# A decoder block on one core: twelve early chunks in the first FFN, activations made ahead of their step, low parts of weighted sums last, and two POOL products on VectorE

## The chip, the cores and the metric

One core of one Trainium2 chip. The metric is the device time of one launch in microseconds, given as the median of several runs. Smaller is better.

## The reference

One layer of a decoder block on 256 tokens of width 2048, in float32. Everything is computed from `x`, a condition `c` and weights:

```python
ada = silu(c) @ w_ada + b_ada          # nine rows of 2048: shift, scale and gate of three sub-layers
h = rms_norm(x) * g * (1 + sc1) + sh1
x = x + 0.5 * gt1 * ((silu(h @ w_gate) * (h @ w_up)) @ w_down)      # first FFN, inner width 5632
u = rms_norm(x) * g * (1 + sc2) + sh2
q, kv, gate_logits, q_r, k_r, v_r, g_r, ga, gb = split(u @ w_in)
merged = sigmoid(ga) * (nsa(q, kv, gate_logits) @ w_proj_nsa) \
       + sigmoid(gb) * (retention(q_r, k_r, v_r, g_r) @ w_proj_ret)
x = x + gt2 * (merged @ w_out)
# second FFN like the first, with sh3, sc3, gt3
```

`nsa` is attention of 16 heads in 4 groups with compressed, selected and window branches; `retention` has 8 heads with 128x256 states, a normalisation over each head's 256 values and a gate `silu(g_r)`.

## The kernel before

Products are made in two parts each: a float32 matrix is split into a high part (`whi`, `ahi`, rounded by ScalarE) and a low part (`wlo`, `alo`, the difference, made by VectorE), and three matmuls add high·high, high·low and low·high. Weights come as tiles of two blocks of 128 rows by 512 columns, 512 KB each. One such tile is a **unit**: `unit` (or the body of `early`) multiplies it with the two halves of the 256 tokens in 12 matmuls of 128x512 (lines 235 to 237, in the early steps 681 to 683).

All loads stand in one written-out list, the **stream**, of weight tiles ("w") and of tiles of `w_ada` ("a"). `run` walks the list. SP issues the loads in that order into six `raw` buffers; a buffer comes free when its tile is prepared. `prep` prepares a tile up to `AHEAD` = 4 stream items before its turn: for "w" ScalarE makes `whi` (line 136) and VectorE `wlo` (line 137), with four buffers of each; for "a" VectorE multiplies by a condition column and adds (line 368, 16 such tiles make the sums of one slice). An item "do" runs a function at its place; a "bar" holds preparation back until the walk has reached it. `push` and `soon` put small pieces into a queue of which one is run after each unit.

The scale and shift of the first FFN come from `w_ada`, so its activations are not known at the start. The kernel therefore goes through the inner dimension in four **steps** (`STEPS`) of four blocks of 128. Step i needs the scale and shift of its own four blocks only. In each step the first `EARLY` = 9 chunks (gate and up chunks in turn, 512 columns each, two units per chunk and step) are taken as far as the step goes; ScalarE takes their sums out of PSUM (line 694) and puts them back before the next step's part (`seed`, line 700). The sums of chunks 0 to 7 lie in buffers of activations, later ones in `t4` buffers, of which there are six. The 16 "a" tiles of the next step are interleaved with the units of this one, by `SPREAD` = 0.95 over the first 17 of 18 units. At the end of that list stand `turn` (transposes of the normalised `x`, line 777), the sums over partitions with a vector of ones (`done`, line 403), and `mk`, which makes the step's activations: two ScalarE activations per block (lines 796 and 797) and VectorE's low part (line 800).

Ahead of the first step, TensorE runs a few matmuls whose results are not used (`with_raw`, `warm`).

Chunks that are not early, and all later matrices, run through `chunk` over the whole inner dimension. In attention, `pv` multiplies the values with the turned weights; the weights' low parts come from `p_tr` (line 1132, VectorE). In retention, `y` normalises a head's output and multiplies it with the gate (line 1235, POOL); `y_tr` transposes it (line 1248). In the merge, `b_done` multiplies (line 1302, VectorE) and adds (line 1303, POOL); `merge` then transposes the sum (line 473, a helper).

Of the kernel before, what the change touches and what calls it, by code (L numbers as in the profile page):

```python
# [29 lines left out]
O_KV, O_GL = 2048, 5120  # L30
O_QR, O_KR, O_VR, O_GR, O_GA, O_GB = 5168, 6192, 7216, 9264, 11312, 13360

RAW, PREP, AHEAD, T4, T2, EARLY, SPREAD = (6, 4, 4, 6, 8, 9, 0.95)
SLOPES = [2.0 ** (-8.0 * (i + 1) / HEADS) for i in range(HEADS)]


LEAD = (0, 0)
BAR = 1
WARM = (10, 15, 4)
FILL = (4, 40, 320, 50, 60, 10)  # L40
SLOW = 6
HOLD = (2,2,1)
# [26 lines left out]
def block_kernel(ctx: ExitStack, tc: tile.TileContext, I, konst, decay, out):  # L69
# [10 lines left out]
    def act_hi(dt=F32R):  # L80
        return ap_.tile([P, 4, S], dt, tag="ahi", name="ahi")
# [57 lines left out]
    def run():  # L139
# [55 lines left out]
        for it in items:  # L195
            kind = it[0]
            if kind == "do":
                it[1]()
                continue
            if kind == "bar":  # L200
                bars.pop(0)
                few = SLOW if len(it) > 2 else 0
                continue
            done = 0
            while st["prep"] < len(stream) and st["prep"] <= at + AHEAD and (not bars or st["prep"] < bars[0]):
                nxt = st["prep"]
                if nxt not in raws or (stream[nxt][0] == "w" and st["w"] >= nw - len(held) + PREP):
                    break
                if few and done == 2:
                    break  # L210
                done += stream[nxt][0] == "w"
                prep()
            few = max(few - 1, 0)
            while late_lo and late_lo[0][0] <= at and kind == "w":
                next_lo()
            if kind == "w":
                it[4](*parts.pop(at))
                nw += 1
# [164 lines left out]
        nc.tensor.matmul(ps, ones_r, by_turns(lo[:, i]), start=False, stop=True)  # L383
        return halves(ps)

    def ada_cols(lay, k0, nk=4, first=False):

        ks = slice(k0, k0 + nk)

# [7 lines left out]
            nc.vector.scalar_tensor_tensor(o[:, 1], o[:, 1], 1.0, g_norm[:, lay, ks], op0=ALU.add, op1=ALU.mult)  # L397

        def done(acc):
            if first:  # L400
                ps = mx()
                for k in range(2 * nk):
                    nc.tensor.matmul(ps[:, k:k + 1], acc[:, k * P:(k + 1) * P], ones[:, 0:1], start=True, stop=True)
                finish(ps[:, 0:2 * nk].rearrange("p (i k) -> p i k", i=2))
                return
            hi, lo = in_parts(acc)

            def f():
# [219 lines left out]
    def ffn(l, his, los, last, first=None, head=None):  # L628
# [79 lines left out]
        if first:  # L708
            its += first(*STEPS[0])
            for i, (k0, nk) in enumerate(STEPS):  # L710
                nxt = [None if i == 0 else ci for ci in range(1, EARLY)] + [0 if i + 1 < len(STEPS) else None]
                w = [it for ci in range(EARLY) for it in early(ci, k0, nk, nxt[ci])]
                if i + 1 < len(STEPS):
                    w = interleave(w, first(*STEPS[i + 1]), int(len(w) * SPREAD), *LEAD)
                its += w
        def both(c):
            g = [] if first and 2 * c < EARLY else chunk(act, src(wg, c), KT, NCH, gate_done(c), head=None if c else head)
# [33 lines left out]
    h1, l1 = [], []  # L751

    def first(k0, nk):
        banks = []

        def scaled(ks):
            for t in range(2):
                nc.scalar.activation(xs[:, t, ks], x[:, t, ks], AF.Copy, scale=rx[:, t:t + 1])

        def warm():  # L760
            ps = mx()
# [3 lines left out]
        def with_raw(raw):  # L765
            nc.tensor.matmul(mx(), ones, raw[:, :NCH], start=True, stop=True)

        def turn():

            ks = slice(k0 * P, (k0 + nk) * P)  # L770
            if k0 == 0:
                scaled(ks)
            for k in range(nk):
                if k % 2 == 0:
                    banks.append(mx([P, 2, S]))
                for t in range(2):
                    nc.tensor.transpose(banks[-1][:, k % 2, t * P:(t + 1) * P],
                                        xs[:, t, (k0 + k) * P:(k0 + k + 1) * P], ident)
            if k0 == 0:
                for n in range(1, 4):  # L780
                    scaled(slice(n * NCH, (n + 1) * NCH))

        def mk():
            n = 1 if k0 == 0 else 2
            if k0 == 0:
                warm()
            for k in range(0, nk, n):
                h32 = t2([P, 2, S])
                for i in range(n):
                    kt = k0 + k + i  # L790
                    if kt % 4 == 0:
                        h1.append(act_hi())
                        l1.append(act_lo())
                    a, b = mod[:, 1, kt:kt + 1], mod[:, 0, kt:kt + 1]
                    xT = banks[(k + i) // 2][:, (k + i) % 2]
                    nc.scalar.activation(h1[-1][:, kt % 4], xT, AF.Identity, scale=a, bias=b)
                    nc.scalar.activation(h32[:, i], xT, AF.Identity, scale=a, bias=b)
                next_lo()
                ks = slice((k0 + k) % 4, (k0 + k) % 4 + n)
                nc.vector.tensor_tensor(l1[-1][:, ks], h32[:, :n], h1[-1][:, ks].bitcast(F32), op=ALU.subtract)  # L800
        o = ada_cols(0, k0, nk, True)
        if k0 == STEPS[1][0]:
            o.insert(5, ("do", load_more))
        if k0 == 0:
            then = {0: lambda raw: small_cols(), 2: lambda raw: rms_first(), 3: lambda raw: turn()}
            then.update({i: with_raw for i in range(*WARM[:2])})
            for i, f in then.items():
                o[i] = (*o[i][:4], lambda raw, f=f, g=o[i][4]: (g(raw), f(raw)))
            o = [("do", lambda: [square(t, n, xs[:, t, n * NCH:(n + 1) * NCH]) for t in range(2) for n in range(4)])] + o
            return o + [("do", mk), ("bar", BAR)]  # L810
        o.insert(len(o) - 1, ("do", turn))
        return o + [("do", mk)]

    def squared(xa, rs):
        def f(t, n):
# [166 lines left out]
    def attention(g):  # L982
# [153 lines left out]
        def pv(t, brs, cmp_):  # L1136
            def f():
# [1 line left out]
                if start:  # L1139
                    box["o", t] = mx()  # L1140
                ps = box["o", t]
                for br in brs:
                    for j in range(t + 1):
                        ph, pl = box["pT", br, t, j]
                        vh, vl = box["v"][:, 0, j, br], box["v"][:, 1, j, br]
                        nc.tensor.matmul(ps, vh, ph, start=start, stop=False)
                        nc.tensor.matmul(ps, vh, pl, start=False, stop=False)
                        nc.tensor.matmul(ps, vl, ph, start=False, stop=False)
                        start = False
                if cmp_:  # L1150
                    nc.tensor.matmul(ps, vc[0:CMP, g, :], by_turns(box["pcT"][0:CMP, t]), start=False, stop=True)
# [27 lines left out]
    def retention(qd):  # L1179
# [35 lines left out]
        def y(h):  # L1215
            def f():
# [15 lines left out]
                for t in range(2):  # L1232
                    nc.vector.tensor_scalar(yn[:, t], ps[:, t], mv[:, t, 0:1], rs[:, t:t + 1],
                                            op0=ALU.subtract, op1=ALU.mult)
                nc.gpsimd.tensor_tensor(yn, yn, G[:, :, vh], op=ALU.mult)
                box["y", h] = yn
            return f

# [58 lines left out]
    def b_done(n):  # L1297
        def f(ps):
            g = sgb.pop(n)
            a = A[0][:, :, n * NCH:(n + 1) * NCH]  # L1300
            for t in range(2):
                nc.vector.tensor_tensor(in_two(g[:, t]), halves(ps[t]), in_two(g[:, t]), op=ALU.mult)
            nc.gpsimd.tensor_tensor(a, a, g, op=ALU.add)  # L1303
        return f

    for n in range(4):
# [58 lines left out]
```

## Time and profile before

| | us |
|---|---|
| median of 3 runs | 2477.15 (2477.02 to 2477.69) |
| the profiled execution, its own time | 2472.4 |
| its span, first to last instruction | 2470.6 |
| PE busy | 2428.3 |
| PE's weight loads busy | 2113.0 |
| DVE (VectorE) busy | 1742.2 |
| ACT (ScalarE) busy | 1202.1 |
| POOL (GpSimd) busy | 169.9 |

All rows and times inside the kernel are of the one profiled execution and count from its span's start. Matmuls are pipelined: a row's duration overlaps the next, so the spacing of starts tells the pace. "Idle before" is the time in which an engine did nothing before an instruction, with what ended it.

### The profile page before, as it was taken

The numbers are of one execution on the slowest core, as the hardware profiler recorded it, in microseconds if no ns is written. First come the engines' busy times: TensorE is split into PE (matmuls) and PEld (weight loads), VectorE is DVE, ScalarE is ACT, GpSimd is POOL, SyncE is SP. The second block draws the span as 40 slices with busy tenths as digits, with TensorE's granted clock in tenths as the row PEclk, the third lists the DMA queues.
The fourth block names the chain that finished last, engine by engine and source line by source line (L and its number), as shares of the span: only waits on it lengthen the run. The fifth ranks groups of instructions, "written<-read, shape, count | busy, mean of one in ns | idle before, by whom it ended". The sixth has DMA issues, their size and how long they took to land. (4 is left out here: it accounts for less than half of the span.)

```text
span 2470.6 us, 31644 instructions
## 1 busy us (share of the span) xinstructions
PE 2428.3 (98%) x11614; PEld 2113.0 (86%) x11614; DVE 1742.2 (71%) x2032; ACT 1202.1 (49%) x1548; POOL 169.9 (7%) x146
## 2 busy tenths in 40 slices
PE   6999999999999999999999999999999999999999
PEld 4888888888888888888888888888888888888887
DVE  7887768998756478886667777777788555555555
ACT  4677444434445455564444444445644444444443
POOL 1000000110000111100000101001000010001001
PEclk9999999999999999999999999999999999999999
DMA  9998888899876455668888787886599666666664
GB/s 352 353 355 293 279 296 296 310 318 343 273 229 203 140 155 160 204 203 272 281 267 256 253 254 254 274 271 232 176 348 325 200 203 203 196 200 202 202 199 152
DMA packets 348264, 616.65 MB, mean 250 GB/s; under 512 B 22096, under 2 KB 79926, under 8 KB 347852
## 3 DMA queue, kind: packets, MB, share of 16 engines
q1 hardware_dynamic: 347852, 614.51, 75.6%
q8 instruction: 91, 1.49, 0.2%
q14 instruction: 65, 0.53, 0.1%
q0 software_dynamic: 256, 0.12, 0.0%
HBM read 612.45 MB, written 2.10 MB: 249 GB/s over the span
## 5 line engine op out<-in xcount | busy, mean ns | idle before, releaser
L137 DVE TENSOR_TENSOR wlo<-raw,whi 128x1024 fp32r<-128x1024 f32 x852 | 1059.2, 1251 | 575.5 <-ACT whi L136 570.7
L136 ACT ACTIVATE whi<-raw 128x1024 fp32r<-128x1024 f32 x852 | 894.7, 1056 | 946.1 <-PE accb L237 717.3
L235 PE MATMUL accb<-whi,ahi 128*128 128x512 f32 x3168 | 1211.8, 383 | 1.3 <-ACT ahi L530 0.9
L236 PE MATMUL accb<-wlo,ahi 128*128 128x512 f32 x3168 | 1201.9, 379 | 1.5 <-DVE wlo L179 0.9
L237 PE MATMUL accb<-whi,alo 128*128 128x512 f32 x3168 | 1201.6, 379 | 0.0
L236 PEld LDWEIGHTS accb<-wlo,ahi 128*128 128x128 f32 x3168 | 599.0, 189 | 87.8 <-DVE wlo L179 3.8
L237 PEld LDWEIGHTS accb<-whi,alo 128*128 128x128 f32 x3168 | 598.7, 189 | 87.3 <-DVE alo L549 1.7
L235 PEld LDWEIGHTS accb<-whi,ahi 128*128 128x128 f32 x3168 | 598.9, 189 | 84.9 <-ACT ahi L530 2.0
L368 DVE SCALAR_TENSOR_TENSOR aacc<-raw,cond,aacc 128x1024 f32<-128x1024 f32 x270 | 353.9, 1311 | 1.4 <-DMA raw<-in_w_ada_dram 0.4
L619 POOL TENSOR_TENSOR x<-x,t 128x512 f32<-128x512 f32 x50 | 80.8, 1636 | 1396.6 <-DVE t L614 1001.0
L682 PE MATMUL accb<-wlo,ahi 128*128 128x512 f32 x288 | 112.4, 390 | 3.0 <-DVE wlo L137 3.0
L683 PE MATMUL accb<-whi,alo 128*128 128x512 f32 x288 | 109.7, 381 | 2.1 <-DVE alo L800 2.1
L681 PE MATMUL accb<-whi,ahi 128*128 128x512 f32 x288 | 110.3, 383 | 0.2
L682 PEld LDWEIGHTS accb<-wlo,ahi 128*128 128x128 f32 x288 | 54.6, 190 | 17.7 <-DVE wlo L137 10.9
L683 PEld LDWEIGHTS accb<-whi,alo 128*128 128x128 f32 x288 | 54.6, 189 | 10.3 <-DVE alo L800 3.3
L681 PEld LDWEIGHTS accb<-whi,ahi 128*128 128x128 f32 x288 | 54.7, 190 | 8.9 <-ACT whi L136 1.0
L598 DVE TENSOR_TENSOR alo<-mx,ahi 128x512 fp32r<-128x512 f32 x52 | 33.5, 686 | 29.3 <-ACT ahi L597 29.1
L597 ACT ACTIVATE ahi<-mx 128x512 fp32r<-128x512 f32 x52 | 28.2, 595 | 48.9 <-PE mx L473 48.9
L614 DVE TENSOR_TENSOR t<-accb,gt 128x512 f32<-128x512 f32 x56 | 36.5, 684 | 9.0 <-PE accb L237 9.0
L640 ACT ACTIVATE t<-accb 128x512 f32<-128x512 f32 x44 | 26.2, 600 | 27.2 <-PE accb L237 22.9
L868 ACT ACTIVATE t<-accb 128x512 f32<-128x512 f32 x44 | 25.9, 596 | 23.3 <-PE accb L237 23.3
L1108 ACT ACTIVATE t<-t,m 128x256 f32<-128x256 f32 (+1 forms) x64 | 28.2, 444 | 18.4 <-DVE m L1099 18.4
(200 smaller groups left out, 1052.9 us busy)
## 6 DMA issues: line engine op xcount, KB each, us to landing
raw<-in_w_ada_dram SPq DMA_DIRECT2D x288, 512.0 KB, 5.5
raw<-in_w_ffn_gate_dram SPq DMA_DIRECT2D x176, 512.0 KB, 5.0
raw<-in_w_ffn_up_dram SPq DMA_DIRECT2D x176, 512.0 KB, 4.7
raw<-in_w_ffn_down_dram SPq DMA_DIRECT2D x176, 512.0 KB, 4.4
raw<-in_w_in_dram SPq DMA_DIRECT2D x176, 512.0 KB, 4.5
raw<-in_w_in_dram SPq DMA_DIRECT2D x128, 256.0 KB, 3.9
raw<-in_w_proj_nsa_dram SPq DMA_DIRECT2D x32, 512.0 KB, 5.4
raw<-in_w_proj_ret_dram SPq DMA_DIRECT2D x32, 512.0 KB, 5.3
```

Source lines behind the costliest of these rows:

```text
L136: nc.scalar.activation(hi_ap, raw_ap, AF.Copy)
L137: nc.vector.tensor_tensor(lo_ap, raw_ap, hi_ap.bitcast(F32), op=ALU.subtract)
L235: nc.tensor.matmul(ps[t], xh, wh, start=kt == 0, stop=False)
L236: nc.tensor.matmul(ps[t], xh, wl, start=False, stop=False)
L237: nc.tensor.matmul(ps[t], xl, wh, start=False, stop=kt == K - 1)
L368: nc.vector.scalar_tensor_tensor(box[0], raw, k, box[0], op0=ALU.mult, op1=ALU.add)
L598: nc.vector.tensor_tensor(lo[:, 2 * b:2 * b + 2], ps, h.bitcast(F32), op=ALU.subtract)
L614: nc.vector.tensor_tensor(in_two(y), halves(ps[t]), in_two(gt[:, n * NCH:(n + 1) * NCH]), op=ALU.mult)
L619: engine.tensor_tensor(xs, xs, y, op=ALU.add)
L681: nc.tensor.matmul(ps[t], xh, wh, start=kt + a == 0, stop=False, **kw)
L682: nc.tensor.matmul(ps[t], xh, wl, start=False, stop=False, **kw)
L683: nc.tensor.matmul(ps[t], xl, wh, start=False, stop=kt + a == k0 + nk - 1, **kw)
```

## The change

Six edits. (1) `EARLY` goes from 9 to 12. (2) The "a" tiles of the next step are spread over all but the last `REST` = 4 units of a step. (3) `mk` is gone: in steps 1 to 3 the activations are made in pieces that `soon` runs after the following units, and the scaling of `x` and its transposes (`turn`) stand after the 8th and 12th "a" tile. (4) In the first step the activations are made block by block with one stream item prepared between two blocks (the new item "prep"). One more `with_raw` is issued. (5) `pv` takes high·high and low-value·high of all tiles first and the products with the weights' low parts last. (6) The product with the gate in `y` and the sum in `b_done` are issued to VectorE instead of POOL.

```diff
-RAW, PREP, AHEAD, T4, T2, EARLY, SPREAD = (6, 4, 4, 6, 8, 9, 0.95)
+RAW, PREP, AHEAD, T4, T2, EARLY, REST = (6, 4, 4, 6, 8, 12, 4)
-WARM = (10, 15, 4)
+WARM = (10, 16, 4)
...
+            if kind == "prep":
+                if st["prep"] in raws:
+                    prep()
+                continue
...
         def done(acc):
-            if first:
+            def by_ones():
                 ps = mx()
                 for k in range(2 * nk):
                     nc.tensor.matmul(ps[:, k:k + 1], acc[:, k * P:(k + 1) * P], ones[:, 0:1], start=True, stop=True)
                 finish(ps[:, 0:2 * nk].rearrange("p (i k) -> p i k", i=2))
+            if then is not None:
+                by_ones()
+                soon(*then)
                 return
...
-                    w = interleave(w, first(*STEPS[i + 1]), int(len(w) * SPREAD), *LEAD)
+                    w = interleave(w, first(*STEPS[i + 1]), len(w) - REST, *LEAD)
...
+        def whole(k, n):
+
+            h32 = t2([P, 2, S])
+            for i in range(n):
+                kt = k0 + k + i
...
+                nc.scalar.activation(h1[-1][:, kt % 4], xT, AF.Identity, scale=a, bias=b)
+                nc.scalar.activation(h32[:, i], xT, AF.Identity, scale=a, bias=b)
+            boxes.append((h32, (k0 + k) % 4, n, h1[-1], l1[-1]))
+
+        def low():
+            h32, k, n, hi, lo = boxes.pop(0)
+            nc.vector.tensor_tensor(lo[:, k:k + n], h32[:, :n], hi[:, k:k + n].bitcast(F32), op=ALU.subtract)
+
+        def at_first(k):
+            if k == 0:
                 warm()
+            whole(k, 1)
+            next_lo()
+            low()
...
+            for k in range(nk):
+                o += [("do", lambda k=k: at_first(k)), ("prep",)]
+            return o[:-1] + [("bar", BAR)]
+        then = [lambda: whole(0, 2), lambda: (low(), whole(2, 2)), low] if nk == 4 else [lambda: whole(0, 2), low]
+        o = ada_cols(0, k0, nk, then)
+        o.insert(12, ("do", turn))
+        o.insert(8, ("do", scaled))
...
-                for br in brs:
-                    for j in range(t + 1):
-                        ph, pl = box["pT", br, t, j]
-                        vh, vl = box["v"][:, 0, j, br], box["v"][:, 1, j, br]
-                        nc.tensor.matmul(ps, vh, ph, start=start, stop=False)
-                        nc.tensor.matmul(ps, vh, pl, start=False, stop=False)
-                        nc.tensor.matmul(ps, vl, ph, start=False, stop=False)
+                tiles = [(br, j) for br in brs for j in range(t + 1)]
+                for i, part in ((0, 0), (1, 0), (0, 1)):
+                    for br, j in tiles:
+                        nc.tensor.matmul(ps, box["v"][:, i, j, br], box["pT", br, t, j][part], start=start, stop=False)
                         start = False
...
-                nc.gpsimd.tensor_tensor(yn, yn, G[:, :, vh], op=ALU.mult)
+                nc.vector.tensor_tensor(yn, yn, G[:, :, vh], op=ALU.mult)
...
-            nc.gpsimd.tensor_tensor(a, a, g, op=ALU.add)
+            nc.vector.tensor_tensor(a, a, g, op=ALU.add)
```

## Rows read from the trace of the kernel before

**Rows 1.** The page, its first part: busy time of each engine, the share of the span, and the number of instructions.

```profile
PE 2428.3 (98%) x11614; PEld 2113.0 (86%) x11614; DVE 1742.2 (71%) x2032; ACT 1202.1 (49%) x1548; POOL 169.9 (7%) x146
```

**Rows 2.** Busy time by stretch. Columns: the stretch and its length in us; busy us and number of instructions of PE, PEld, DVE, ACT and POOL; granted clock (1.00 is full), busy share of the DMA engines, GB/s.

```profile
36.76:88.62 51.86, 49.73 (x230) 40.63 (x228) 43.28 (x40) 30.98 (x43) 0.00 (x0) 0.99 1.01 368
88.62:140.21 51.59, 50.72 (x242) 42.55 (x242) 42.13 (x39) 40.27 (x63) 0.00 (x0) 1.00 0.96 344
140.21:191.71 51.50, 50.60 (x242) 42.71 (x242) 41.85 (x39) 40.35 (x63) 0.00 (x0) 1.00 0.96 350
...
250.00:312.00 62.00, 62.00 (x289) 54.28 (x288) 44.60 (x41) 27.17 (x29) 0.00 (x0) 1.00 0.84 283
```

**Rows 3.** Waits of the weight loads of TensorE (PEld) from 36 to 212 us. Columns after the names: us in total, times, longest us.

```profile
PEld accb L682 <- DVE wlo L137: 10.9, 30, 1.1
PEld accb L683 <- DVE alo L800: 3.3, 3, 1.8
```

**Rows 4.** TensorE's matmuls in order of time, at the boundaries of the steps. Columns: start us, duration us, engine, line, output and inputs, shape, count; idle time before it and who ended it in brackets. L681 to L683 are the units of the steps, L777 the transposes of x, L403 the sums over partitions, L473 the first transposes of the last step.

```profile
36.76 0.63 PE L681 MATMUL accb<-whi,ahi 128*128 128x512 f32 x1
...
86.04 1.04 PE L777 MATMUL mx<-kc,xs 128*128 128x128 f32 x8
86.91 1.84 PE L403 MATMUL mx<-ones,aacc 128*128 128x1 f32 x16
88.62 0.46 PE L681 MATMUL accb<-whi,ahi 128*128 128x512 f32 x1
...
137.63 1.04 PE L777 MATMUL mx<-kc,xs 128*128 128x128 f32 x8
...
140.21 0.46 PE L681 MATMUL accb<-whi,ahi 128*128 128x512 f32 x1
...
189.13 1.04 PE L777 MATMUL mx<-kc,xs 128*128 128x128 f32 x8
...
191.71 0.46 PE L681 MATMUL accb<-whi,ahi 128*128 128x512 f32 x1
...
196.55 0.48 PE L683 MATMUL accb<-whi,alo 128*128 128x512 f32 x1 [1.40 <-DVE alo L800]
...
211.76 1.04 PE L473 MATMUL mx<-kc,t 128*128 128x128 f32 x8
```

**Rows 5.** The start of the first step: one stretch as in rows 2, then rows in order of time of TensorE and ScalarE.

```profile
34.70:38.10 3.40, 3.40 (x11) 2.74 (x11) 2.32 (x5) 2.56 (x6) 0.00 (x0) 0.51 1.05 389
...
40.29 0.48 PE L681 MATMUL accb<-whi,ahi 128*128 128x512 f32 x1
...
41.61 0.48 PE L682 MATMUL accb<-wlo,ahi 128*128 128x512 f32 x1 [0.83 <-DVE wlo L137]
...
39.15 2.98 ACT L136 ACTIVATE whi<-raw 128x1024 fp32r<-128x1024 f32 x3
```

**Rows 6.** Groups of instructions by line and shape, ScalarE and VectorE, 36 to 250 us. Columns after the count: busy us, mean ns of one; idle time before them and its releasers.

```profile
L136 ACT ACTIVATE whi<-raw 128x1024 fp32r<-128x1024 f32 x76 | 80.4, 1068 | 46.2 <-DMA raw<-in_w_ffn_gate_dram 21.5 <-DMA raw<-in_w_ffn_up_dram 16.1 <-PE accb L683 4.1
L700 ACT ACTIVATE accb<-alo 128x512 f32<-128x512 f32 x24 | 13.7, 606 | 2.7 <-DVE t L647 2.7
...
L694 ACT ACTIVATE ahi<-accb 128x512 f32<-128x512 f32 x24 | 13.1, 600 | 1.6 <-PE accb L683 1.6
...
L137 DVE TENSOR_TENSOR wlo<-raw,whi 128x1024 fp32r<-128x1024 f32 x75 | 91.2, 1223 | 21.8 <-ACT whi L136 21.3
L368 DVE SCALAR_TENSOR_TENSOR aacc<-raw,cond,aacc 128x1024 f32<-128x1024 f32 x55 | 70.3, 1278 | 0.4 <-DMA raw<-in_w_ada_dram 0.4
```

**Rows 7.** The first product of weights and values of an attention group, TensorE and then VectorE in order of time; and the waits of TensorE on the same low parts over the whole span.

```profile
913.31 0.38 PE L1146 MATMUL mx<-t,t 128*128 128x512 f32 x1
914.15 0.48 PE L1147 MATMUL mx<-t,t 128*128 128x512 f32 x1 [0.47 <-DVE t L1132]
...
913.42 1.28 DVE L1132 TENSOR_TENSOR t<-mx,t 128x512 fp32r<-128x512 f32 x2
...
PE mx L1147 <- DVE t L1132: 1.5, 4, 0.5
```

**Rows 8.** Retention, end of one head pair: POOL and TensorE in order of time; and the waits of the weight loads for POOL's product over the whole span.

```profile
1375.22 2.12 POOL L1235 TENSOR_TENSOR t<-t,t 128x512 f32<-128x512 f32 x1 [1.18 <-DVE t L1233]
...
1379.60 4.45 POOL L1235 TENSOR_TENSOR t<-t,t 128x512 f32<-128x512 f32 x1 [1.18 <-DVE t L1233]
...
1384.11 0.66 PE L1248 MATMUL mx<-kc,t 128*128 128x128 f32 x4 [0.29 <-POOL t L1235]
...
PEld mx L1248 <- POOL t L1235: 1.2, 2, 0.7
```

**Rows 9.** The last merge: TensorE, VectorE and POOL in order of time; and one group of VectorE over the whole span, as in rows 6.

```profile
1675.38 0.38 PE L237 MATMUL accb<-whi,alo 128*128 128x512 f32 x1
...
1677.96 0.38 PE L237 MATMUL accb<-whi,alo 128*128 128x512 f32 x1
1679.20 1.09 PE L473 MATMUL mx<-kc,A 128*128 128x128 f32 x8 [0.86 <-POOL A L1303]
...
1676.88 3.35 DVE L137 TENSOR_TENSOR wlo<-raw,whi 128x1024 fp32r<-128x1024 f32 x1 [0.17 <-ACT whi L136]
...
1676.79 2.35 POOL L1303 TENSOR_TENSOR A<-A,t 128x1024 f32<-128x1024 f32 x1 [41.70 <-DVE t L1302]
...
L619 DVE TENSOR_TENSOR x<-x,t 128x512 f32<-128x512 f32 x6 | 4.1, 689 | 0.1
```

More of the change, by code (lines that the diff above doesn't have):

```diff
@@ L384, in over_partitions, with ada_cols @@
         return halves(ps)
-    def ada_cols(lay, k0, nk=4, first=False):
+    def ada_cols(lay, k0, nk=4, then=None):
         ks = slice(k0, k0 + nk)
@@ L753, in first, with scaled, turn @@
     def first(k0, nk):
-        banks = []
-        def scaled(ks):
+        banks, boxes = [], []
+        def scaled():
+            ks = slice(k0 * P, (k0 + nk) * P)
             for t in range(2):
                 nc.scalar.activation(xs[:, t, ks], x[:, t, ks], AF.Copy, scale=rx[:, t:t + 1])
+        def turn():
+            for k in range(nk):
+                if k % 2 == 0:
+                    banks.append(mx([P, 2, S]))
+                for t in range(2):
+                    nc.tensor.transpose(banks[-1][:, k % 2, t * P:(t + 1) * P],
+                                        xs[:, t, (k0 + k) * P:(k0 + k + 1) * P], ident)
         def warm():
@@ L766, in with_raw @@
             nc.tensor.matmul(mx(), ones, raw[:, :NCH], start=True, stop=True)
[L768 to L781, printed above, removed]
@@ L783, in mk @@
-        def mk():
-            n = 1 if k0 == 0 else 2
-            if k0 == 0:
-                warm()
[L787 to L800, printed above, removed]
@@ L801, in first @@
-        o = ada_cols(0, k0, nk, True)
-        if k0 == STEPS[1][0]:
-            o.insert(5, ("do", load_more))
+        def whole(k, n):
+            h32 = t2([P, 2, S])
+            for i in range(n):
+                kt = k0 + k + i
+                if kt % 4 == 0:
+                    h1.append(act_hi())
+                    l1.append(act_lo())
+                a, b = mod[:, 1, kt:kt + 1], mod[:, 0, kt:kt + 1]
+                xT = banks[(k + i) // 2][:, (k + i) % 2]
+                nc.scalar.activation(h1[-1][:, kt % 4], xT, AF.Identity, scale=a, bias=b)
+                nc.scalar.activation(h32[:, i], xT, AF.Identity, scale=a, bias=b)
+            boxes.append((h32, (k0 + k) % 4, n, h1[-1], l1[-1]))
@@ L804, in first @@
+        def low():
[3 more added lines that the diff above has]
+            if k == 0:
+                warm()
+            whole(k, 1)
+            next_lo()
+            low()
         if k0 == 0:
-            then = {0: lambda raw: small_cols(), 2: lambda raw: rms_first(), 3: lambda raw: turn()}
+            o = ada_cols(0, k0, nk, ())
+            then = {0: lambda raw: small_cols(), 2: lambda raw: rms_first(), 3: lambda raw: (scaled(), turn())}
@@ L809, in first @@
             o = [("do", lambda: [square(t, n, xs[:, t, n * NCH:(n + 1) * NCH]) for t in range(2) for n in range(4)])] + o
-            return o + [("do", mk), ("bar", BAR)]
-        o.insert(len(o) - 1, ("do", turn))
-        return o + [("do", mk)]
+            for k in range(nk):
+                o += [("do", lambda k=k: at_first(k)), ("prep",)]
[4 more added lines that the diff above has]
+        o.insert(8, ("do", scaled))
+        if k0 == STEPS[1][0]:
+            o.insert(5, ("do", load_more))
+        return o
     def squared(xa, rs):
```

## The prediction

> **What bounds the kernel now.** I read the page first, for shares: TensorE is busy 98% of the span [rows 1]. A busy row of matmuls overlaps its neighbours, so that number hides gaps. The pace is read from starts instead: in a fed stretch 12 matmuls of 128x512 start in 1677.96 - 1675.38 = 2.58 us, 0.2157 us each when taken over longer stretches [rows 9]. One unit (a 512 KB load of weights and its 12 matmuls) therefore takes 2.59 us of TensorE, and time can be won only where matmuls start later than that.
>
> Second, the stages. From 36.8 to 191.7 us, three steps of 18 units each with 16 loads of w_ada between them, the DMA engines are 96 to 101% busy and move 344 to 368 GB/s; a fed stretch later (250 to 312 us) has 84% and 283 GB/s [rows 2]. Third, the waits of the weight loads in 36 to 212 us: 10.9 us on a wlo that VectorE had not made, 3.3 us on an activation's low part, against 1.0 us on a whi and no others over 0.3 us [rows 3]. wlo comes after whi, whi after the landed load, so the first is mostly the DMA's lateness seen through two engines.
>
> Fourth, the boundaries in order of time give the size of it [rows 4]. Matmuls of units between 36.76 and 86.04: 17 units, 204 x 0.2157 = 44.00 of 49.28 us, 5.28 lost. 88.62 to 137.63: 216 matmuls, 46.59 of 49.01, 2.42 lost. 140.21 to 189.13: 48.92, 2.33 lost. 191.71 to 211.76: 84 matmuls, 18.12 of 20.05, 1.93 lost. Together **11.96 us**; between steps stand 2.58 us of transposes and column sums that the change keeps. The largest single hole is the 1.4 us before 196.55, where the first unit of a step waits for the activations' low part that VectorE makes only then.
>
> **Part 1: twelve early chunks.** A step goes from 18 to 24 units, so 34 loads per step become 40. TensorE then needs 24 x 2.588 + 2.58 = 64.7 us per step and the loads need 40 x 0.524 MB = 20.97 MB: 324 GB/s, below all three measured rates of 344 to 368 [rows 2]. The 16 loads of w_ada are now spread over 20 units instead of 17 (24 less 4): 36 loads in 20 x 2.588 + 2.58 = 54.3 us ask for 347 GB/s, just at the measured rates, and the last 4 units ask for 4 loads in 10.4 us, which refills the six raw buffers. Before, 17 units with 16 loads asked for 33 in 46.6 us, 371 GB/s, over the lower two of the rates, hence the waits. So steps 1 and 2 should run without waits, and step 0 nearly.
>
> Nothing is added to TensorE; weights are loaded once either way. ScalarE gets more: three more chunks have their sums taken out and put back. Per chunk of two units (5.18 us) it does two whi at 1.07, two evacuations and two seeds at about 0.6 [rows 6]: at most 4.6 us, plus, per step, eight activations and two scalings that are no larger, 10 x 0.6 / 12 = 0.5 per chunk. That is the load per unit that it has today, and what covers it is that two units stay prepared ahead. VectorE: per unit 1.22 + 0.8 x 1.28 = 2.25 of 2.59 us [rows 6], where it was 1.22 + 0.94 x 1.28 = 2.42.
>
> One cover may go. The sums of chunks 8 to 11 take four of the six t4 buffers, the row of the first gate's bias a fifth, the first gate chunk's result in the last step the sixth. The second gate chunk needs a seventh two units before the first is turned. It must wait for those transposes, 0.87 us of TensorE right behind the unit (as 86.04 to 86.91 in [rows 4]): at four such places ScalarE stands about 1 us each, below the 5.18 us of prepared work, so I price it at nothing; without the cover it costs up to 4 us.
>
> **Part 2: activations over the last four units.** With the last load of w_ada due at unit 20, the sums come there and the eight ScalarE activations follow in two halves behind units 21 and 22, the low parts behind 22 and 23; the next step starts after 24. The 3.3 us of waits on the low part [rows 3] go, and ScalarE no longer makes whi wait behind eight activations at the very place where the step starts. These are inside the 11.96.
>
> In the first step the loads' preparation is threaded through four activation pieces. Today whi of the second unit runs only at 39.15, behind all eight activations; TensorE starts the second unit at 40.29 and waits for wlo until 41.61 [rows 5]. After it, whi can run behind four activations, at about 37.4, its wlo ends near 39.7, and the unit starts at about 39.9. But the second low parts and a w_ada step now sit in VectorE's queue between: the last low part moves to about 41.8, where TensorE wants it at 41.0, a new wait of about 0.8. The unit ends some 0.6 us earlier than before (43.4 for 44.0). The one more idle matmul with a raw tile (16 for 15) comes before the column sums, while TensorE idles; the clock was at the lower level from 34.7 to 38.1 (0.51) [rows 5], and if one more activity keeps it up, the first matmuls gain up to 0.6. I take 0.
>
> What stays of the 11.96: about 2 at the start (1.4 to 2.6), 0.7 through step 0, nothing after. **Term: 9.2 us gained** (bounds 4, if only the low-part waits and the start go, and 11.5).
>
> **Part 3: low products last.** In each of four groups the second matmul of the weighted sum over values waits for a low part: hi product at 913.31, the next matmul at 914.15, just behind the first of two low parts, where 913.53 was possible: 0.63 lost, of which the view of waits counts 0.47; it counts 1.5 in four waits, so with 0.16 more each some 2.1 us are lost in all [rows 7]. Now four matmuls that need no low part come first (to 914.17), then the first low one, which is ready, then the second, whose low part ends at 913.42 + 1.28 = 914.70: it would start at 914.39 and starts at 914.75, 0.36 lost. Gain 0.27; the other groups have the same two low parts of 0.64 each behind each other, so the same: **1.1 us** (bounds 0 and 2.1).
>
> **Part 4: POOL's work to VectorE.** Retention: POOL's multiplication lasts from 1379.60 to 1384.05 and the transposes start at 1384.11; of the 1.2 us that the weight loads idle at two such places, about 0.75 is loss, the rest the 0.2 us by which loads are spaced anyway [rows 8]. On VectorE the same shape with both inputs in SBUF takes 0.69 [rows 9], so the tile is ready near 1380.3. **Gain 0.75** (0 to 0.8). Merge: the last matmul starts at 1677.96, the transposes could follow at 1678.18 and do at 1679.20 because POOL adds until 1679.14. An operation of 128x1024 on VectorE takes 1.22 to 1.28 [rows 6]; begun where POOL begins, at 1676.79, it is done at 1678.05, in time. **Gain 1.0** (0 to 1.0). The price is 8 x 0.69 + 4 x 1.24 = 10.5 us in VectorE's queue, ahead of wlo. But today VectorE already stands while POOL works: the wlo at 1676.88 takes 3.35 us instead of 1.22 [rows 9], and POOL's 2.12 becomes 4.45 beside VectorE [rows 8]. So of the price at least 2.1 us is paid already at the last merge, and I take the rest as covered by two prepared units.
>
> The Trainium skill, page "SBUF — State Buffer", section "Who interferes with whom", says that a VectorE instruction with two SBUF inputs and a GpSimd instruction that reads SBUF exclude each other for the whole instruction. The row of 3.35 us agrees; by that rule each merge frees VectorE about 1.1 us earlier than now, so the 10.5 would be under zero net at the merges; the sum does not use it.
>
> **Sum**: 9.2 + 1.1 + 0.75 + 1.0 = 12.05 us. The profiled execution took 2472.4 us (span 2470.6), 4.75 below the median of the runs, and becomes 2460.35; the median becomes 2477.15 - 12.05 = **2465.1 us**.
>
> **Rivals.** (a) *Half the early gain.* 347 GB/s is at the edge; if the loads keep to 344, and the low end of the measured rates holds in each 20 units, the last unit's wlo remains just late and 4 to 5 us come instead of 9.2: 2477.15 - 7.4 = 2469.7. For it: the 0.96 share at 344 GB/s. Against: the four units without w_ada, and that the next step starts from full buffers. (b) *The early gain does not appear*: whatever holds TensorE there is not the loads but the chain whi, wlo behind evacuations and seeds, which keeps its weight per unit; parts 3 and 4 alone: 2474.3, within the noise bound. Against: DMA 96 to 101% busy and ScalarE's queue idle for loads. (c) *Slower*: ScalarE's order decides. There are 48 chunk passes instead of 36, and at each an evacuation waits for TensorE with whi queued behind it, now together with the activation halves and the t4 waits. If a pass costs TensorE 0.5 us, 48 x 0.5 = 24 replaces 11.96: 2477.15 + 12.0 - 2.85 = 2486.3; from 0.31 us per pass on the kernel is slower. Against: after 197 us, with the same chunks and no w_ada, the units run at pace. (d) The VectorE operations of part 4 expose wlo: up to 10.5 lost, 2465.1 + 10.5 = 2475.6, same as now; against it, the 3.35 us that wlo takes today.
>
> **How the numbers follow.** Chances: main 0.60 (own range 2462 to 2468), (a) 0.22, (b) 0.07, (d) 0.05, (c) 0.06. The range reaches from the main case with every bound kind (11.5 + 1.1 + 0.8 + 1.0 + 0.6 = 15, 2462) to (a), with a little beyond at both ends: 2461 to 2472. Five microseconds are 0.2%, about what a measurement tells from no change. Faster by more: 0.60 + 0.22 + a little of (b) and (d), 0.84; same: 0.11; slower: 0.05.
>
> **What would show it.** Right: steps of about 64.7 us, with DMA share down to about 0.9; waits on wlo in the early steps under 3 us in all and none on the low part after the first step; the four waits in the value products halved; none before the transposes of retention's and the last merge's. Wrong: ScalarE idle on TensorE with whi queued, waits on wlo at every chunk, t4 waits in the last step, or new wlo waits between 1300 and 1680 us.

## The result, and the profile after

| | us |
|---|---|
| median before, on the same chip | 2477.11 (6 runs, 2474.24 to 2477.69) |
| median after | 2463.14 (6 runs, 2462.47 to 2464.39) |
| ratio of after to before | 0.9946, 95% interval 0.9933 to 0.9959 |
| the profiled execution after, its own time and its span | 2464.18 and 2462.4 |

The change is faster by 14.0 us between the medians, 0.54%; forecast were 2465.1 us and 12.05 us of gain. In two further comparisons, below, the changed kernel gained 12.85 and 13.57 us over the kernel before.

The stretches of the changed kernel, with columns as in [rows 2]: the first three are its steps 0, 1 and 2, each up to the first unit behind the sums over partitions. These sums now come four units before a step's end, so the first stretch has 20 units and the next two have 24 each. The last two stretches lie in the first FFN's down product, where the scale and shift of the second norm are loaded.

```profile
37.37:93.26 55.89, 55.48 (x265) 48.08 (x264) 46.20 (x42) 37.95 (x51) 0.00 (x0) 0.99 1.02 370
93.26:158.08 64.82, 64.82 (x314) 57.05 (x314) 48.82 (x44) 53.50 (x82) 0.00 (x0) 1.00 0.93 326
158.08:222.91 64.83, 64.83 (x314) 57.06 (x314) 49.65 (x45) 53.51 (x83) 0.00 (x0) 1.00 0.93 327
420.00:450.00 30.00, 30.00 (x141) 26.27 (x140) 26.72 (x24) 13.72 (x14) 6.13 (x4) 1.00 0.98 350
450.00:530.00 80.00, 77.01 (x369) 66.29 (x368) 72.71 (x97) 33.17 (x36) 10.40 (x7) 1.00 0.86 293
```

Steps 1 and 2 take 64.82 and 64.83 us for 24 units, where the working gave 64.7 for a step without waits, and the DMA engines have come down from 0.96 to 0.93 busy and from 344 and 350 to 326 and 327 GB/s.

The waits of the weight loads on wlo and on low parts in 37 to 250 us, as [rows 3]: 14.2 us before, 1.3 after, all of it in the first step.

```profile
PEld accb L690 <- DVE alo L802: 0.8, 1, 0.8
PEld accb L689 <- DVE wlo L137: 0.5, 2, 0.3
```

The start of the first step, VectorE, ScalarE and then TensorE in order of time, to be read against [rows 5]:

```profile
39.06 1.23 DVE L137 TENSOR_TENSOR wlo<-raw,whi 128x1024 fp32r<-128x1024 f32 x1 [0.43 <-ACT whi L136]
40.20 0.42 DVE L802 TENSOR_TENSOR alo<-t,ahi 128x256 fp32r<-128x256 f32 x1
40.54 1.28 DVE L372 SCALAR_TENSOR_TENSOR aacc<-raw,cond,aacc 128x1024 f32<-128x1024 f32 x1
41.73 0.42 DVE L802 TENSOR_TENSOR alo<-t,ahi 128x256 fp32r<-128x256 f32 x1
...
37.96 1.07 ACT L136 ACTIVATE whi<-raw 128x1024 fp32r<-128x1024 f32 x1
...
42.21 0.48 PE L690 MATMUL accb<-whi,alo 128*128 128x512 f32 x1 [0.41 <-DVE alo L802]
```

The second unit's `whi` now runs between the activations, at 37.96 instead of 39.15, and the last low part waits behind a step of w_ada in VectorE's queue and ends at 42.15, so that a matmul that could start at 41.64 starts at 42.21: the new wait of the working, 0.57 us here where 0.8 was forecast (0.78 in the second profile of the changed kernel, in which TensorE had the full clock here).

The last merge, TensorE and VectorE in order of time, to be read against [rows 9]. The transposes (line 480) follow the last matmul at once, and wlo takes 1.22 us where it took 3.35.

```profile
1671.18 0.38 PE L241 MATMUL accb<-whi,alo 128*128 128x512 f32 x1
1671.40 1.04 PE L480 MATMUL mx<-kc,A 128*128 128x128 f32 x8
...
1669.96 1.22 DVE L1315 TENSOR_TENSOR A<-A,t 128x1024 f32<-128x1024 f32 x1
1671.11 1.22 DVE L137 TENSOR_TENSOR wlo<-raw,whi 128x1024 fp32r<-128x1024 f32 x1
```

In the tables below, **early loss** is what [rows 4] gave for the kernel before: for each run of units from the first one on, the time to the next boundary less 0.2157 us for each matmul, added up to the end of the last step's first 7 to 10 units. It was 11.96 there, and is 2.1 in the changed kernel.

### The profile page after: what moved, and what is told of

Same layout as the page of the kernel before. It is cut to its first block, busy times and chain, and to the rows that moved or that the text cites. A ratio compares the mean times of both kernels' runs of the same rounds, so it can differ in the third digit from the quotient of the medians.

```text
span 2462.4 us, 31664 instructions
## 1 busy us (share of the span) xinstructions
PE 2425.2 (98%) x11616; PEld 2116.0 (86%) x11616; DVE 1738.0 (71%) x2044; ACT 1219.8 (50%) x1584; POOL 139.8 (6%) x134
## 4 chain that ended last, share of the span: by engine, by line
PE 88%; DVE 6%; DMA 3%; issue 2%; ACT 1%; POOL 0%; SPq 0%; DVEq 0%; ACTq 0%
PE accb L240 24%; PE accb L241 24%; PE accb L239 24%; PE accb L690 3%; PE accb L688 3%; PE accb L689 3%; DVE wlo L137 2%; DVE aacc L372 2%; DMA raw<-in_w_ffn_down_dram 2%; PE mx L480 1%; DMA raw<-in_w_ada_dram 1%; PE mx L923 1%; PE mx L1160 1%; ACT whi L136 1%; PE mx L1108 0%
## 5 line engine op out<-in xcount | busy, mean ns | idle before, releaser
L137 DVE TENSOR_TENSOR wlo<-raw,whi 128x1024 fp32r<-128x1024 f32 x852 | 1048.6, 1240 | 581.9 <-ACT whi L136 576.2
L690 PEld LDWEIGHTS accb<-whi,alo 128*128 128x128 f32 x384 | 72.7, 189 | 11.1 <-DVE alo L802 0.8
L689 PEld LDWEIGHTS accb<-wlo,ahi 128*128 128x128 f32 x384 | 72.7, 189 | 10.6 <-DVE wlo L137 0.5
L621 DVE TENSOR_TENSOR t<-accb,gt 128x512 f32<-128x512 f32 x56 | 36.2, 684 | 7.8 <-PE accb L241 7.8
```

Of the source, the lines that this page charges most:

```text
L137: nc.vector.tensor_tensor(lo_ap, raw_ap, hi_ap.bitcast(F32), op=ALU.subtract)
L621: nc.vector.tensor_tensor(in_two(y), halves(ps[t]), in_two(gt[:, n * NCH:(n + 1) * NCH]), op=ALU.mult)
L689: nc.tensor.matmul(ps[t], xh, wl, start=False, stop=False, **kw)
L690: nc.tensor.matmul(ps[t], xl, wh, start=False, stop=kt + a == k0 + nk - 1, **kw)
```

## The experiments

All medians below are of 5 to 11 runs, with the kernel before run beside them on the same chip.

**Where the loss of the kernel before varies.** The profiled execution of before lay 4.75 us under its median, so the kernel before was profiled once more, unchanged.

> The kernel before, unchanged, profiled once more. Its first profiled execution (2472.4 us) lay 4.7 us under its median, so the trace shows less loss than most executions have. If the extra loss sits where loads bound TensorE (theory: loads), this profile shows more than 11.96 us lost between the first unit and 212 us, and the rest of the trace the same within 1 us. Rival: the start before the first unit (36.76 us) differs, or the loss is spread over the span.

Measured: 2475.81 us, the profiled execution 2475.91. Its steps:

```profile
36.15:89.68 53.53, 50.02 (x228) 40.13 (x229) 44.22 (x41) 31.96 (x44) 0.00 (x0) 1.00 1.01 361
89.68:141.18 51.50, 50.77 (x243) 42.55 (x242) 41.07 (x39) 39.18 (x62) 0.00 (x0) 1.00 0.96 343
141.18:193.86 52.68, 50.82 (x243) 42.63 (x242) 42.52 (x39) 40.88 (x64) 0.00 (x0) 1.00 0.95 343
```

53.53 us in step 0 where [rows 2] have 51.86, and 52.68 in step 2 where they have 51.50: the early loss is 14.8 us instead of 11.96. Of the 3.5 us between the two spans (2474.1 and 2470.6) that is 2.8; the down product's stretch from 440 to 530 us adds 0.6 and retention another 0.5, and the first unit starts 0.6 us earlier. So most of what sets these two executions of one kernel apart lies in the steps that the loads bound, and the execution on which the sum was made was one of little loss.

**The parts alone.** The changed kernel with its late parts undone, as the diff shows, and the kernel before with the same lines changed the other way:

```diff
-                for i, part in ((0, 0), (1, 0), (0, 1)):
-                    for br, j in tiles:
-                        nc.tensor.matmul(ps, box["v"][:, i, j, br], box["pT", br, t, j][part], start=start, stop=False)
+                for br in brs:
+                    for j in range(t + 1):
...
+                        nc.tensor.matmul(ps, vh, ph, start=start, stop=False)
+                        nc.tensor.matmul(ps, vh, pl, start=False, stop=False)
+                        nc.tensor.matmul(ps, vl, ph, start=False, stop=False)
...
-                nc.vector.tensor_tensor(yn, yn, G[:, :, vh], op=ALU.mult)
+                nc.gpsimd.tensor_tensor(yn, yn, G[:, :, vh], op=ALU.mult)
...
-            nc.vector.tensor_tensor(a, a, g, op=ALU.add)
+            nc.gpsimd.tensor_tensor(a, a, g, op=ALU.add)
```

> The changed kernel with parts 3 and 4 undone: value products in the old order, the retention product and the merge sum on POOL again. Theory: the early part carries most of the gain, so 2.0 to 2.9 us slower than the changed kernel, 2465 to 2466.5. If VectorE's added operations cost what they bring (new wlo waits of 0.6 at 1382 and 1514 us in the changed kernel), under 1.5 us slower. Rival: parts 3 and 4 carry more than half, 2470 or more.

> The kernel before with parts 3 and 4 alone. Theory: 2.0 to 2.9 us under the kernel before, about 2474.5. If the parts add up, this gain and that of the early part alone sum to the 14 us of the whole.

Measured: early part alone 2464.24, late parts alone 2473.32, the kernel before 2475.96 beside them. The early part alone gains 11.7 us, the late parts alone 2.6. Together that is 14.3, and the whole gained 12.9 to 14.0 in three comparisons: the parts add up to about the whole, and the early one carries four fifths. A later run of the changed kernel on the same chip has 2462.24 (below), so the late parts bring 2.0 on top of the early one. The late gain was as expected (2.0 to 2.9); the early part ended 0.8 us under the range expected of it.

**How many chunks.** The changed kernel with `EARLY` 9 and 10 for 12, everything else as changed:

> The changed kernel with 9 early chunks instead of 12; the activations are still made over the last four units. Theory loads: 34 loads per step ask for 362 GB/s over TensorE's 49.2 us, and 30 in the first 14 units for 405; the steps stay bound by the loads at about 51 us, wlo waits stay, the low-part waits (3.3 us) go: 2469 to 2473. Rival activations: the order of the activations won the time, so it stays within 2 us of the changed kernel, 2463 to 2465.

> The changed kernel with 10 early chunks. A step then asks for 36 loads in 20 x 2.588 + 2.58 = 54.3 us, 347 GB/s, at the measured rates of 344 to 368. Theory loads: most of the loss of 9 chunks (10.8 us) goes, 2 to 5 us stay, 2464 to 2466.5 where the changed kernel has 2463. Rival: the gain grows evenly by chunk, then a third of the way from 9 to 12, about 8 us lost and 2468.

| early chunks | loads a step asks for, GB/s | early loss, us | median, us | before on the same chip |
|---|---|---|---|---|
| 9 | 362 | 10.6 | 2470.02 | 2475.96 |
| 10 | 347 | 4.7 | 2463.93 | 2476.08 |
| 12 | 324 | 2.6 | 2463.23 | 2476.08 |

The early loss of 12 is that of a second profile of the changed kernel, run beside 10 chunks:

> The changed kernel, unchanged, beside the others on one chip. About 12 to 14 us under the kernel before; early loss (first unit to the first transposes of the last step) 2 to 3 us, and 3 to 4 us lost between 440 and 530 us, where the kernel before lost 1.2 and 1.8 in two profiles, if that loss comes with the change rather than by chance.

Measured: 2463.23 us, and 3.1 us lost between 440 and 530 us, as expected. Step 1 of the two other kernels, 9 chunks first:

```profile
80.94:132.79 51.85, 50.35 (x243) 43.20 (x242) 41.78 (x39) 40.38 (x63) 0.00 (x0) 1.00 0.97 348
```

```profile
84.69:139.17 54.48, 54.48 (x266) 47.89 (x266) 43.72 (x40) 43.91 (x69) 0.00 (x0) 1.00 0.98 349
```

Both move 348 to 349 GB/s with DMA engines 97 to 98% busy. With 9 chunks the step needs 49.2 us of TensorE and takes 51.85; with 10 it needs 54.3 and takes 54.48. Steps 1 and 2 together lose 4.5, 0.5 and 0.2 us with 9, 10 and 12 chunks, so for them the knee stands about where the asked rate falls to the one seen here; what 10 chunks still lose is in step 0 (3.9 us). Against the kernel before beside each, 9 chunks gain 5.9 us, 10 gain 12.15 and 12 gain 12.85, so one chunk of the three brings six of the seven microseconds.

**One cost taken away.** Nine chunks again, with half of each w_ada tile of steps 1 to 3 not loaded:

```diff
+                elif stream[i][0] == "a" and 16 <= st["a"] < 64:
+                    nc.sync.dma_start(dst[:, 0:1], src[:, 0:1])
...
-                fn(raw[:, :nk * n])
+                fn(raw[:, None, :n].to_broadcast([P, 2, n]) if half else raw[:, :nk * n])
```

> The kernel with 9 early chunks again (10.8 us lost early, 2470.0), with one cost taken away: of each w_ada tile of steps 1 to 3 only the half with the shifts is loaded and VectorE reads it for both halves, so the scales are left out of the computation; every instruction of the engines stays. A step then asks for 26 loads' worth in 49.2 us, 277 GB/s. Theory loads: the early loss falls under 4 us, 2463 to 2465. Rival: the chain whi, wlo on ScalarE and VectorE holds TensorE with 9 chunks, and the loss stays at 9 to 11 us.

Measured: 2464.69 us, 11.1 under the kernel before beside it; with all loads, 9 chunks stood 5.9 under it. Waits of the weight loads on wlo, 42 to 215 us, with 9 chunks and all loads, then with half:

```profile
PEld accb L689 <- DVE wlo L137: 7.3, 10, 1.1
```

```profile
PEld accb L696 <- DVE wlo L137: 4.0, 5, 0.9
```

Steps 1 and 2 lose 0.75 and 0.46 us instead of 2.68 and 1.79, with the same instructions on every engine. Step 0 still loses 4.27 us where it lost 5.74, in both kernels some 1.3 of it matmuls that took 0.21 us more each at the lower clock (below), so the early loss, 5.8, missed the expected "under 4". The rival, the chain of `whi` and `wlo`, is out for steps 1 and 2; for step 0 the loads are part of the loss, not shown to be all of it.

**The place of the activations.** Twelve chunks, with the activations made at once before the last unit:

```diff
-RAW, PREP, AHEAD, T4, T2, EARLY, REST = (6, 4, 4, 6, 8, 12, 4)
+RAW, PREP, AHEAD, T4, T2, EARLY, REST = (6, 4, 4, 6, 8, 12, 1)
...
-                soon(*then)
+                for f in then:
+                    f()
```

> Twelve chunks with the activations made all at once at the old place, right before the last unit of a step (w_ada spread over 23 of 24 units). Theory: the low-part waits of steps 1 to 3 come back, 0.5 to 1.6 us each as in the kernel before, so 2 to 4 us slower than the changed kernel, 2465 to 2467. Rival: with twelve chunks enough is prepared ahead and the place is worth nothing, within 0.7 us.

Measured: 2463.30 us where the changed kernel beside it has 2463.23. Of the waits on the low part, 3.3 us in [rows 3], about half come back: these two between 42 and 215 us, and one more of 0.8 us at 233 us:

```profile
PEld accb L691 <- DVE alo L803: 0.8, 2, 0.4
```

The early loss is 3.8 us, 1.2 more than in the profile of the changed kernel beside it; the times do not show it. So the rival holds by the time: with twelve chunks the place of the activations is worth 1.2 us in a profile and nothing that the medians can tell. That it is because more is prepared when the step starts was not measured.

**The retention product back on POOL.** One line of the diff undone, beside a third run of the changed kernel:

> The changed kernel with the retention product on POOL again. If the move brought the 0.75 us of the prediction, 0.75 slower, with waits before the transposes of retention and none on wlo. If it traded one wait for another (0.64 and 0.67 us on wlo appear right behind in the changed kernel), the sum of both kinds between 1290 and 1530 us differs by under 0.5 us and the time stays the same.

> The changed kernel unchanged, beside these three on one chip: 2462.5 to 2464.5, 2 to 3 us lost early, 3 to 3.7 us between 440 and 530 us.

Measured: 2464.13 with POOL, 2462.24 without, 0.3 under what was expected of it, with 3.7 us lost early and 3.9 between 440 and 530 us, both more than expected. Waits of the weight loads, 1290 to 1530 us, with POOL first and then the changed kernel's first profile:

```profile
PEld mx L1260 <- POOL t L1247: 2.5, 4, 0.7
PEld accb L240 <- DVE wlo L137: 1.3, 2, 1.1
```

```profile
PEld accb L240 <- DVE wlo L137: 1.8, 2, 0.9
```

Waits of both kinds are there, so neither of the two expectations holds. The move took 2.5 us of waits before the transposes away and left 1.8 on wlo, 0.5 more than with POOL: 2.0 us by these waits. From the same matmul to the same matmul retention takes 1.4 us less with the product on VectorE, in times 1.9 with runs that overlap. In the kernel before, the waits for POOL's product were fewer [rows 8]: against its two profiles the changed kernel's retention loses 0.2 us and gains 0.3. Why the changed kernel with POOL waits there more than the kernel before was not tried.

**What is lost later.** The changed kernel loses 3.6 us between 440 and 530 us (3.1 and 3.9 in the other two profiles), the kernel before 1.2 and 1.8, counting starts that come more than about 0.1 us late. Two things were tried on it. First all residual sums on VectorE:

```diff
-            plus(by_gate(ps, n, t), n, t, nc.vector if last and n == 3 else nc.gpsimd)
+            plus(by_gate(ps, n, t), n, t, nc.vector)
```

> The changed kernel with all residual additions to x (line 626) on VectorE instead of POOL. In the changed kernel two wlo take 3.44 us for 2.35 where POOL adds, and 3.6 us are lost between 440 and 530 us. Theory exclusion: VectorE gives 0.69 per addition and gets back 1.1 to 1.6, so the loss there falls below 2.5 us and the kernel gains 0.5 to 2 us. Rival: VectorE's queue is what is full there (0.93 busy), the additions come on top, 1 to 3 us slower.

Measured: 2462.57 us beside 2463.23, with runs that overlap; the loss there 2.3 us. The rival's 1 to 3 us slower did not come; that the time gained is not shown. But the waits on wlo between 430 and 545 us, 2.6 us in the changed kernel beside it, are down to this, with every load at its old place:

```profile
PEld accb L240 <- DVE wlo L137: 1.2, 2, 0.8
```

Then the loads of that stretch: the second number of `FILL` says how many items before the end of the list the last of them is due, and 28 spreads them over 12 more. With it goes one change at the start: of the three preparations of loads between the four pieces of the activations, the third comes only behind the last piece:

```diff
-FILL = (4, 40, 320, 50, 60, 10)
+FILL = (4, 28, 320, 50, 60, 10)
...
-                o += [("do", lambda k=k: at_first(k)), ("prep",)]
-            return o[:-1] + [("bar", BAR)]
+                o += [("do", lambda k=k: at_first(k))] + [("prep",)] * (k < 2)
+            return o + [("bar", BAR)]
```

> The changed kernel with two sizes moved: the w_ada loads of the second norm are spread over all but the last 28 units of their stretch instead of 40 (64 loads in 108 units ask for 322 GB/s instead of 338), and the third load prepared between the first step's activations goes behind the fourth. Theory loads: the 3 to 3.6 us lost between 440 and 530 us fall under 1.5; the wait of 0.6 to 0.8 on the low part at 41 us goes: 2460 to 2461.5. Rival: the loss at 450 to 530 us is VectorE's queue behind residual sums and turned chunks, and stays: 2462.5 or more.

Measured: **2460.70 us** (2460.14 to 2460.84), ratio to the kernel before 0.9939 (0.9925 to 0.9952), 1.5 us under the changed kernel beside it, whose runs all lie higher (2461.12 to 2464.52). Waits of the weight loads from 430 to 545 us, the changed kernel and then this one:

```profile
PEld accb L240 <- DVE wlo L137: 3.0, 4, 1.5
PEld accb L241 <- DVE alo L605: 1.6, 1, 1.6
PEld accb L239 <- ACT ahi L604: 0.5, 1, 0.5
```

```profile
PEld accb L241 <- DVE alo L605: 1.5, 1, 1.5
PEld accb L239 <- ACT ahi L604: 0.5, 1, 0.5
```

All waits on wlo are gone, and at 420 to 450 us the DMA engines go from 350 to 329 GB/s. But every w_ada item that moves is a load and a step of 1.28 us in VectorE's queue, so this run does not separate the two. What stays is the wait on the low parts of the chunks that are turned there; so the loss falls to 1.7, not under the expected 1.5. The wait on the low part at 41 us is gone too, but that is not shown to come from the edit: here TensorE had the lower clock until 40.0 us, and in the third profile of the changed kernel, where it had it until 39.6, only 0.3 us of that wait was there.

## Why the prediction was right, and where it was not

**The bound and the rate were read rightly.** The forecast compared the rate that a step asks for with the rate that [rows 2] show delivered, and put steps 1 and 2 at 64.7 us without waits; they take 64.82 and 64.83, and the DMA share is 0.93 where 0.9 was forecast. The number of chunks and the halved loads show the same cause from two sides, in steps 1 and 2; in step 0 the loads are shown to be a part of it. The waits for t4 buffers, priced at nothing, cost nothing: up to 430 us of the kernel before the changed one gains 9.84 us behind the first unit, and the early loss alone is 9.82 less.

**The term of 9.2 us was too small for a typical execution.** What stays was forecast at 2.7 us and is 2.1 to 3.7 in three profiles. What was there to lose was read from one execution with 11.96; the second profile of the kernel before has 14.8. Early gain between the profiled execution of before and the first one of after: 11.96 - 2.14, less 0.61 for the later first unit (37.37 for 36.76), 9.2 as forecast. Between the second profiles of both, 14.8 - 2.6 = 12.2, less 0.2 for it. The profiled execution lay 4.75 us under the median of the runs; the sum went over to the median as if the loss were the same there. That step failed, by about 3 us.

**Part of the nearness is luck.** Between the two executions that were profiled first the gain is 8.2 us (spans of 2470.6 and 2462.4), not 12.05, as 2.8 us were given back in the down product and retention brought nothing. Between the medians it is 14.0, as most executions of the kernel before had more to lose early. These errors pull opposite ways, and the forecast lies nearer to the median than its terms do.

**Half of part 2 does little.** The low-part waits were put down to the activations' place; with twelve chunks about half of them go whatever the place, and the other half costs 1.2 us in a profile and nothing that the medians show. The term as a whole held since both edits are in it.

**Part 3** gave what the working says. The row that ends the six products of [rows 7] in the kernel before, and then the six and what follows them in the changed kernel:

```profile
915.34 1.04 PE L1127 MATMUL mx<-kc,t 128*128 128x128 f32 x8
```

```profile
907.03 2.00 PE L1160 MATMUL mx<-t,t 128*128 128x512 f32 x6
908.86 1.04 PE L1142 MATMUL mx<-kc,t 128*128 128x128 f32 x8
```

From 913.31 to 915.34 is 2.03 us for six, from 907.03 to 908.86 is 1.83, where the pace of 0.2157 needs 1.29. So 0.20 is gained in this group; forecast were 0.27. Of the 0.54 left, 0.38 is one wait, where 0.36 was forecast. Over the whole of attention, from the same matmul to the same matmul, the kernel before takes 340.06 and 340.11 us in two profiles and the changed kernel 339.33 in both: 0.7 and 0.8 us, where 1.1 was forecast. What failed is the step that the other groups gain the same: the third gains 0.04, as its wait was only 0.38 us before and 0.2 comes back on the unit right behind.

**Part 4**: merge 1.0 forecast, 1.0 measured (1677.96 to 1679.20 before, 1671.18 to 1671.40 now). Retention 0.75 forecast, -0.2 and 0.3 found against the two profiles of the kernel before. The wait was taken from the transposes, but the matmuls on wlo at 1382 and 1514 us now start 0.6 and 0.7 us late, where the kernel before had 0.3 at the second alone; such waits were only in the list of what would be wrong and in rival (d), not in the sum. A further 0.35 us that no term has is gained behind the last matmul, only where part 4 is in the kernel; why was not looked into.

**Not in the sum at all**: 1.5 and 2.8 us, counted between the same matmuls in two pairs of profiles, given back around 440 to 530 us. No term of the change lies there. What costs it is not shown. In 420 to 450 us the changed kernel moves 350 GB/s with the DMA engines 0.98 busy; but the kernel before moves 361 at 0.99 in the same part of its work (429 to 459 us) and loses less behind it, and TensorE waits in neither of these stretches, but after them, where the DMA share is 0.80 (450 to 491 us) and 0.92 (491 to 530). `FILL` with 28 for 40 takes the waits on wlo away and the residual sums on VectorE more than half of them, so loads, VectorE's own queue, and VectorE beside POOL are all in question. Why the changed kernel is hit harder there than the one before, with the same list of work from that point on, stays open. With 9 chunks, and the loads and activations placed as changed, 3.1 us are lost there too, with 10 chunks 1.7: the loss does not follow the lead with which a kernel arrives.

The whole sum, from the second profiles of both, each piece between the same matmuls: 12.2 - 0.2 early, + 0.8 attention, + 0.3 retention, + 1.1 merge, + 0.35 behind the last matmul, - 1.5 down product = 13.05 us, against 2475.91 - 2462.92 = 13.0 measured.

**The rivals.** Half the early gain (a) assumed that the 20 units with w_ada must keep up by themselves; with 10 chunks they ask for 381 GB/s in their 16 units and steps 1 and 2 still run, losing 0.5 us. So here the mean over the step counted, and not the 16 units alone. (b) is refuted for steps 1 and 2 by the halved loads, (c) by steps 1 and 2 running at the pace, and (d) shows at two places with 1.3 us in all, 0.3 of it there before.

## What to carry to other kernels

Compare the rate that a stage asks for (bytes over the bound engine's own time) with the rate that the trace shows delivered: a stage just above it loses again and again, and taking a little more work into the stage puts it below. Most of the gain is had at that knee, here after one chunk of three. The stage that waited for loads also varied most between two executions here (2.8 of 3.5 us), so size such a loss from more than one. And a wait that is taken from one place can turn up at the next: measure the stretch between the same two instructions before and after, not the wait.

## What was not expected of the hardware

The delivered rate is not one number: 370 GB/s in 37 to 93 us of the changed kernel with the DMA engines at 1.02 by this view, but 343 to 351 GB/s at 0.95 to 0.98 in the steps after that were bound by loads. Nor is 351 a limit of what can come: the kernel before moved 366 GB/s from 148 to 198 us, across a step's end, and 397 from 1877 to 1894 us, where TensorE did not wait. So 343 to 351 is what steps of this kind got here as a mean, and the rate to plan such a step of this kernel by.

The Trainium skill, page "DMA: Bandwidth & Descriptors", section "Specifications", gives about 358 GB/s as the limit of the memory for a core. The 343 to 351 GB/s of steps 1 and 2 lie under it; the 366 to 397 above do not agree with it. The Trainium skill, page "HBM Reference", section "Specifications (TRN2)", has about 425 GB/s for a core that streams alone. The stretches named here stay below it.

TensorE's clock at the start goes either way without a change in the program. The first unit of the second profile of the changed kernel, and of the kernel with `FILL` 28; in both TensorE had run its column sums from 33.3 us and four more matmuls from 35.1 us before it:

```profile
36.33:39.70 3.37, 3.28 (x12) 2.15 (x13) 2.93 (x5) 3.37 (x7) 0.00 (x0) 1.00 1.04 385
```

```profile
36.32:39.70 3.38, 3.37 (x8) 2.48 (x9) 2.94 (x5) 3.38 (x7) 0.00 (x0) 0.54 1.05 387
```

Twelve matmuls began in the one at the full clock (2.4 GHz) and eight in the other, whose granted clock of 0.54 is 1.2 GHz for nearly all of the stretch: six matmuls took 0.21 us more each, 1.3 us. The third profile of the changed kernel, the same program as the second, had the lower level too (from 36.2 to 39.6 us). It need not cost anything: the two rows' first steps lose 1.98 and 1.97 us up to their transposes, as the first then waits 0.78 us for a low part. Of the 14 profiled executions 8 had the lower level for a stretch that began between 34.5 and 37.1 us and was over by 40.5: one of the three with 15 idle matmuls in front, seven of the eleven with 16. That the sixteenth matmul does anything is not shown; the sum had it at nothing.
